# The first stage of an encoder block: x loaded by channels, and the token norm applied after the q, k, v products

## The chip, the cores and the metric

The kernel runs on one core of a Trainium2 chip. The core has TensorE (PE in the profile; its weight loads are listed as PEld), VectorE (DVE), ScalarE (ACT), GpSimd (POOL), a queue engine that issues most transfers (SyncE, SP), and 16 DMA engines. The metric is the device time of one execution in microseconds (us); the median of several runs is compared.

## The reference

One layer of a hybrid encoder block, on 1024 tokens by 1024 channels, in f32. The part that the change touches is its beginning:

```python
h = rms_norm(x, norm_mix[i])                 # y = x * rsqrt(mean(x*x, over channels) + 1e-6); y * gain
proj = h @ w_in[i]                           # 1024 x 4608
q = proj[..., O_Q:O_K].reshape(bsz, s, ATTN_Q_HEADS, HEAD_DIM)      # 512 columns
k = proj[..., O_K:O_V].reshape(bsz, s, ATTN_KV_HEADS, HEAD_DIM)     # 128 columns
v = proj[..., O_V:O_RWKV].reshape(bsz, s, ATTN_KV_HEADS, HEAD_DIM)  # 128 columns
q = rotary_partial(rms_norm(q, q_norm[i]), positions)
k = rotary_partial(rms_norm(k, k_norm[i]), positions)
```

The other columns of `proj` feed an RWKV-7 scan in both directions and two gates per channel. Windowed attention, the scan, the output products, a squared-ReLU MLP and a gated input embedding follow; the change leaves them as they are.

Since the token's factor rsqrt(mean(x*x)+eps) multiplies a whole row of h, it can as well multiply the row of a product: (x * gain) @ w, times the factor, is h @ w.

## The kernel before

Every product of two f32 matrices is taken in three parts: each operand is split into a high part, rounded to the format F32R, and a low part, the difference; then high by high, high by low and low by high are summed in one PSUM bank. `split` (L187) does it for one tile: a copy on ACT makes the high part, a subtraction on DVE or POOL the low one.

The first stage works on 8 token tiles of 128 tokens (t) and 8 channel tiles of 128 channels (k).

- x is loaded by tokens, one 128x1024 tile `xt` for each t (L330). `norm_tile` (L234) takes the sum of squares along the row with one ACT activation (L237), the factor with a small DVE operation (L172) and a power on POOL (L174), and multiplies the tile by factor and gain on DVE (L245).
- TensorE turns the normed tile to channels by tokens: 8 transposes of 128x128, in two groups of four (`tp`, L253). `split` takes each group out of PSUM into `Hh` and `Hl` (L189, L190), which hold the transposed h for two halves of 512 tokens each. All products with w_in read them.
- The weights of q, k and v, 768 columns, come in 8 slices by k (`wqs`, L335) and are split into `wqh` and `wql`, three of the low parts on POOL (`WQP`), five on DVE.
- Token tile t then takes 48 products `psq` (8 k, 2 halves of 384 columns, 3 parts; L439 to L441). Between them stand, at chosen k, the transposes of tile t+1 and those of q and k of tile t-2 (`heads`, L377; `qtp`, L384).
- The result is copied out of PSUM by ACT (`qkv`, L449), v goes to memory (`va_d`, L450), and q and k get a norm by head: squares on ACT (L453), sums on DVE (L455), a power on POOL (`r2`, L458). `rotated` (L395) multiplies, applies the rotation in six small DVE operations, and splits the result; `heads` transposes it, ACT copies it to `qkT` (L386), and POOL issues the transfers to memory (L388, L390).
- After the eighth tile come the first two column blocks of the RWKV part (z12, z13): four sums of 24 products of 128x512 (L218 to L222), with the last two tiles' `heads` between them. Then the preparation of the scan begins with `keys` (first product L230).

The order in which each engine takes its instructions is drawn up ahead of time from the order of the program and from when inputs are planned to be ready; each engine then works through its list in that order and waits at the head of it. `keep_in_program_order` pins an instruction in its place.

## Time and profile before

| what | us |
|---|---|
| median of 3 runs (lowest, highest) | 1730.46 (1728.19, 1732.09) |
| the profiled execution, first to last instruction | 1724.9 |
| PE busy | 1666.1 |
| DVE busy | 1165.3 |
| ACT busy | 879.8 |
| POOL busy | 123.0 |

Busy time of TensorE counts each matmul from its start to its modelled end, though the next one starts before that end; how dense TensorE is, is read from the distance between starts. A start in the timeline is counted from the first instruction of the execution. Of POOL's 123 us the larger part lies in the first 125 us: eight powers of the head norms (15.9 us), eight of the token norms (4.5 us), three low parts of `wql` (6.2 us), four of `wlo` (5.8 us) and 24 transfers to issue (9.4 and 5.8 us).

### The profile page before, as it was taken

To read this page: it belongs to the slowest core of one execution; us is meant where nothing else is said; L and a number is where in the kernel's file an instruction comes from. 1 tells how busy PE (TensorE), PEld (TensorE's weight loads), DVE (VectorE), ACT (ScalarE), POOL (GpSimd) and SP (SyncE) were. 2 spreads that over 40 slices of the span, in tenths; PEclk is the share of its full clock that TensorE was granted. 3 is DMA by queue.
4 is the path that set the end of the run, shared out by engine and by line. 5 is a ranking of instruction groups with operands and counts; after the bars stand their busy time and mean duration, and the time that the engine had idled before them with its cause. 6 is when DMAs were issued, how large, how long until landed. Compare 5 with 4: busy or idle time off the path is not lost.

```text
span 1724.9 us, 29927 instructions
## 1 busy us (share of the span) xinstructions
PE 1666.1 (97%) x11544; PEld 1344.1 (78%) x11544; DVE 1165.3 (68%) x2055; ACT 879.8 (51%) x1620; POOL 123.0 (7%) x148
## 2 busy tenths in 40 slices
PE   7999999899999999998999999999999999999998
PEld 7987777666577878776778878888888888888887
DVE  6658998166948595976763786766667867685342
ACT  5548887277555646464522454444444444554221
POOL 3430000411210000000000100000000000000000
PEclk9999999999999999999999999999999999999999
DMA  6363666846265544456762335444439874574110
GB/s 219 80 151 104 175 184 176 245 130 170 62 183 150 154 138 130 134 168 194 229 223 69 104 119 172 156 140 153 156 132 343 287 218 143 162 222 150 42 40 37
DMA packets 274238, 269.19 MB, mean 156 GB/s; under 512 B 47920, under 2 KB 196272, under 8 KB 274096
## 3 DMA queue, kind: packets, MB, share of 16 engines
q1 hardware_dynamic: 264160, 254.18, 47.6%
q0 software_dynamic: 9792, 12.59, 2.8%
q8 instruction: 91, 1.49, 0.4%
q10 hardware_dynamic: 144, 0.52, 0.1%
q14 instruction: 51, 0.42, 0.1%
HBM read 186.49 MB, written 80.74 MB: 155 GB/s over the span
## 4 chain that ended last, share of the span: by engine, by line
PE 73%; DVE 13%; DMA 6%; ACT 5%; issue 3%; POOL 1%; SPq 0%; DVEq 0%; ACTq 0%; POOLq 0%
PE ff2ps L1793 18%; PE ff1ps L1541 16%; PE gmm L212 3%; DMA wst<-in_w_in_dram 2%; DVE tmp L808 2%; DVE Z L811 2%; PE plps L222 2%; PE plps L218 2%; PE plps L220 2%; PE mm L230 2%; PE mm L232 2%; PE mm L231 2%; PE uaps L212 1%; PE po L943 1%; PE gps L212 1%
## 5 line engine op out<-in xcount | busy, mean ns | idle before, releaser
L1793 PE MATMUL ff2ps<-th,sl 128*128 128x512 f32 x448 | 174.3, 389 | 0.0
L1793 PE MATMUL ff2ps<-tl,sh 128*128 128x512 f32 x448 | 174.3, 389 | 0.0
L1793 PE MATMUL ff2ps<-th,sh 128*128 128x512 f32 x448 | 173.9, 389 | 0.0
L189 ACT CAST sh<-sst 128x512 fp32r<-128x512 f32 x109 | 67.8, 622 | 104.4 <-PE ff2ps L1793 58.7
L190 DVE TENSOR_TENSOR sl<-sst,sh 128x512 fp32r<-128x512 f32 x109 | 75.2, 689 | 47.2 <-ACT sh L189 46.9
L1541 PE MATMUL ff1ps<-mh,w1h 128*128 128x512 f32 x256 | 100.3, 392 | 1.9 <-ACT w1h L189 1.9
L1541 PE MATMUL ff1ps<-ml,w1h 128*128 128x512 f32 x256 | 99.9, 390 | 0.0
L1541 PE MATMUL ff1ps<-mh,w1l 128*128 128x512 f32 x256 | 99.6, 390 | 0.0
L1793 PEld LDWEIGHTS ff2ps<-th,sh 128*128 128x128 f32 x448 | 84.0, 188 | 17.9 <-ACT th L189 0.3
L1793 PEld LDWEIGHTS ff2ps<-tl,sh 128*128 128x128 f32 x448 | 84.1, 188 | 17.5
L1793 PEld LDWEIGHTS ff2ps<-th,sl 128*128 128x128 f32 x448 | 84.1, 188 | 17.4
L189 ACT CAST whi<-wst 128x512 fp32r<-128x512 f32 x100 | 60.4, 617 | 67.7 <-DMA wst<-in_w_in_dram 37.6
L174 POOL TENSOR_TENSOR rstd<-ms,neghalf 128x1 f32<-128x1 f32 x24 | 14.8, 616 | 924.2 <-DVE ms L172 924.2
L189 ACT CAST w1h<-w1st 128x512 fp32r<-128x512 f32 x48 | 28.3, 620 | 98.8 <-DMA w1st<-in_w_ff_dram 58.9
L190 DVE TENSOR_TENSOR w1l<-w1st,w1h 128x512 fp32r<-128x512 f32 x48 | 31.7, 687 | 50.8 <-ACT w1h L189 50.8
L190 DVE TENSOR_TENSOR wlo<-wst,whi 128x512 fp32r<-128x512 f32 x72 | 48.5, 687 | 22.7 <-ACT whi L189 22.4
L1541 PEld LDWEIGHTS ff1ps<-mh,w1h 128*128 128x128 f32 x256 | 48.1, 188 | 12.9 <-ACT w1h L189 2.8
L218 PE MATMUL gmm<-hh,whi 128*128 128x512 f32 x136 | 55.6, 409 | 2.5 <-ACT whi L189 2.5
L1541 PEld LDWEIGHTS ff1ps<-mh,w1l 128*128 128x128 f32 x256 | 48.1, 188 | 10.8 <-DVE w1l L190 0.6
L222 PE MATMUL gmm<-hh,wlo 128*128 128x512 f32 x136 | 55.5, 408 | 0.5 <-POOL wlo L190 0.5
L1541 PEld LDWEIGHTS ff1ps<-ml,w1h 128*128 128x128 f32 x256 | 48.1, 188 | 10.0
L220 PE MATMUL gmm<-hl,whi 128*128 128x512 f32 x136 | 55.5, 408 | 0.0
(406 smaller groups left out, 4720.7 us busy)
## 6 DMA issues: line engine op xcount, KB each, us to landing
wst<-in_w_in_dram SPq DMA_DIRECT2D x92, 256.0 KB, 3.4
tst<-in_w_ff_dram SPq DMA_DIRECT2D x80, 256.0 KB, 4.1
w1st<-in_w_ff_dram SPq DMA_DIRECT2D x32, 512.0 KB, 5.0
hid_S<-h SPq DMA_DIRECT2D x64, 256.0 KB, 2.1
sst<-hid_S SPq DMA_DIRECT2D x64, 256.0 KB, 2.7
hid_A<-h SPq DMA_DIRECT2D x48, 256.0 KB, 2.3
sst<-hid_A SPq DMA_DIRECT2D x45, 256.0 KB, 3.8
ra_d<-ra SPq DMA_DIRECT2D x8, 1024.0 KB, 5.9
```

The costliest lines, as they stand in the source:

```text
L189: a = nc.scalar.copy(hi, src)
L190: b = (lo_eng or nc.vector).tensor_tensor(out=lo, in0=src, in1=hi.bitcast(F32), op=ALU.subtract)
L212: tc.keep_in_program_order(nc.tensor.matmul(*a, **kw))
L218: mm(ps, ah, bh, start=(i == 0), stop=False)
L220: mm(ps, ah, bl, start=False, stop=False)
L222: mm(ps, al, bh, start=False, stop=(i == n - 1))
L230: nc.tensor.matmul(ps, ah, bh, start=(i == 0), stop=False)
L231: nc.tensor.matmul(ps, ah, bl, start=False, stop=False)
L232: nc.tensor.matmul(ps, al, bh, start=False, stop=(i == n - 1))
L808: nc.vector.tensor_tensor(out=tv, in0=Lp[:, t + 1:32, t:t + 1].broadcast_to([P, n, m]), in1=Z[:, t:t + 1, 0:m].broadcast_to([P, n, m]), op ...
L1541: nc.tensor.matmul(ps, x_[:, k, :], y_[:, k, :], start=start and k + i == 0, stop=k == 3 and i == 2, skip_group_check=True)
L1793: nc.tensor.matmul(banks[bs][i], x_[:, isl], y_, start=fresh and p + j == 0, stop=p == NPR - 1 and j == 2, skip_group_check=True)
```

## The change

x is also laid out by channels on the host (`xT`), and loaded in 16 slices of 128 channels by 512 tokens, so that no transpose of x is left. A slice is multiplied by the gain of its channels alone and split at once (`gained`: high part on ACT, low part on DVE); q, k and v are taken from that. For the first three token tiles (`NA`) the products run by k, all three tiles for one k before the next; the other five run tile by tile (`tile_of`).

The sums of squares come from squares on ACT that are added up over k on POOL (`squared`, into `acc`, which has one buffer for both halves), and four small products with a column of ones per half (`stats`), which give the factor of each token. The factor goes onto v (ACT), into the head norm's mean of squares as its square (`rq`), and into the head norm's factor (`qk_norm`).

z12 and z13 and all later products still take the normed h. For them the factors are put on a diagonal (`dg`, DVE), spread to all partitions by a 128x512 product with ones (`spread`, `rB`), multiplied with x and gain (`scaled`, DVE, reading `rB` from PSUM), and split again into `Hh` and `Hl` (`normed`: ACT, and the low part on POOL for the first half, on DVE for the second).

The q and k transposes of tiles 0 to 2 stand in tiles 5 to 7, those of tiles 3 to 6 in the four sums of z12 and z13, and those of tile 7 behind these. Transposes, sums and `psq` share six PSUM banks.

```diff
@@ -125,6 +125,8 @@
     out = {"pc": np.ascontiguousarray(np.concatenate([cols[n] for n in PC], 0).T)}
     out["wa2"] = np.ascontiguousarray(np.concatenate([a["w2"], a["a2"]], 1).transpose(1, 0, 2))
     out["qkn"] = np.ascontiguousarray(np.concatenate([np.tile(a["q_norm"], 8), np.tile(a["k_norm"], 2), a["sink"]])[None])
+    out["xT"] = np.ascontiguousarray(a["x"].T.reshape(KT, P, T).transpose(1, 0, 2))
+    out["gcol"] = np.ascontiguousarray(a["norm_mix"].reshape(KT, P).T)
...
@@ -321,64 +323,153 @@
     QW = pool(sQ, "wqkv")
     PMM = pool(sMM, "psA", space=PSUM, side="right")
     with ExitStack() as s0:
-        A0 = pool(sA, "x0", bufs=2)
+        A0 = pool(sA, "x0")
         PT0 = pool(s0, "ps0", space=PSUM)
-        xts, wq = [], []
...
+        XT = [A0.tile([P, KT, 512], F32, name="xt0"), PY.tile([P, KT, 512], F32, name="xt1", tag="yk")]
+        acc, wq = [], []
+        gcol = QW.tile([P, KT], F32, name="gcol")
+        nc.scalar.dma_start(gcol, I["gcol"])
+        ones = A0.tile([P, P], F32, name="ones")
+        nc.vector.memset(ones, 1.0)
+        def pinned(ins):
+            tc.keep_in_program_order(ins)
+            return ins
+        def load_x(h, k):
+            nc.sync.dma_start(XT[h][:, k], I["xT"][:, k, 512 * h:512 * h + 512])
+        def gained(h, k):
+            pinned(nc.scalar.activation(out=Hh[h][:, k], in_=XT[h][:, k], func=AF.Copy, scale=gcol[:, k:k + 1]))
+            pinned(nc.vector.scalar_tensor_tensor(out=Hl[h][:, k], in0=XT[h][:, k], scalar=gcol[:, k:k + 1], in1=Hh[h][:, k].bitcast(F32),
+                                                  op0=ALU.mult, op1=ALU.subtract))
+        def squared(h, k):
+            if k == 0:
+                acc.append(A0.tile([P, 512], F32, name="acc", bufs=1))
+                pinned(nc.scalar.activation(out=acc[h], in_=XT[h][:, k], func=AF.Square))
+            else:
+                sq = A0.tile([P, 512], F32, name="sq", bufs=2)
+                pinned(nc.scalar.activation(out=sq, in_=XT[h][:, k], func=AF.Square))
+                nc.gpsimd.tensor_tensor(out=acc[h], in0=acc[h], in1=sq, op=ALU.add)
+        def load_wq(k):
+            st = QW.tile([P, 768], F32, name="wqs", bufs=2) if k % 3 == 0 else QW.tile([P, 768], F32, name="wqs", tag="qkv", bufs=4)
             hi = QW.tile([P, 768], F32R, name=f"wqh{k}")
             lo = QW.tile([P, 768], F32R, name=f"wql{k}")
-            split(hi, lo, st, nc.gpsimd if k in WQP else nc.vector, pin=k < WQPIN)
+            for g in range(2) if k == 0 else (slice(None),):
+                gs = slice(384 * g, 384 * g + 384) if k == 0 else g
+                nc.sync.dma_start(st[:, gs], w_in[:, k, 0:768][:, gs])
+                pinned(nc.scalar.copy(hi[:, gs], st[:, gs]))
+                b = (nc.gpsimd if k in WQP else nc.vector).tensor_tensor(out=lo[:, gs], in0=st[:, gs], in1=hi[:, gs].bitcast(F32), op=ALU.subtract)
+                if k not in WQP:
+                    pinned(b)
             wq.append((hi, lo))

-        load_x(0, nc.sync)
-        ident = const("ident", [P, P])
-        gain = A0.tile([P, DM], F32, name="gain", bufs=1)
-        nc.scalar.dma_start(gain, I["gains"][0:1, :].partition_broadcast(P))
-        def normed(t):
-            xs = norm_tile(A0, xts[t], gain, t, 1 if t else 2, pin=t in SQPIN)
+        NA = 3
+        pss = {}
+        def psq_k(t, k):
             h, tq = divmod(t, 4)
             tsl = slice(tq * P, (tq + 1) * P)
...
-        first = normed(0)
+            if k == 0:
+                pss[t] = [PT0.tile([P, 384], F32, name="psq", tag="psq", bufs=6) for _ in range(2)]
+            ah, al = Hh[h][:, k, tsl], Hl[h][:, k, tsl]
+            for g in range(2):
+                gs = slice(384 * g, 384 * g + 384)
+                nc.tensor.matmul(pss[t][g], ah, wq[k][0][:, gs], start=(k == 0), stop=False)
+                nc.tensor.matmul(pss[t][g], al, wq[k][0][:, gs], start=False, stop=False)
+                nc.tensor.matmul(pss[t][g], ah, wq[k][1][:, gs], start=False, stop=(k == KT - 1))
+        rs, rq = [], []
+        def stats(h):
+            st = PMM.tile([P, 4], F32, name="st", tag="mm", bufs=2)
+            for i in range(4):
+                nc.tensor.matmul(st[:, i:i + 1], acc[h][:, i * P:(i + 1) * P], ones[:, 0:1], start=True, stop=True)
+            ms, r, q = (QW.tile([P, 4], F32, name=n, bufs=2) for n in ("ms", "rx", "rq"))
+            nc.vector.tensor_scalar(out=ms, in0=st, scalar1=1.0 / DM, scalar2=EPS, op0=ALU.mult, op1=ALU.add)
+            nc.gpsimd.tensor_tensor(out=r, in0=ms, in1=neghalf.broadcast_to([P, 4]), op=ALU.pow)
+            nc.vector.scalar_tensor_tensor(out=q, in0=r, scalar=1.0 / 64, in1=r, op0=ALU.mult, op1=ALU.mult)
+            rs.append(r)
+            rq.append(q)
+        rB = {}
+        dgs = {}
+        def dg(h):
+            dgs[h] = A0.tile([P, 4, P], F32, name="dg", tag="sq", bufs=2)
+            nc.vector.tensor_tensor(out=dgs[h], in0=ident.unsqueeze(1).broadcast_to([P, 4, P]), in1=rs[h].unsqueeze(2).broadcast_to([P, 4, P]), op=ALU.mult)
+        def spread(h):
+            rB[h] = PMM.tile([P, 512], F32, name="rB", tag="mm", bufs=2)
+            nc.tensor.matmul(rB[h], ones, dgs[h].rearrange("p a t -> p (a t)"), start=True, stop=True)
+        def scaled(h, ks):
+            for k in ks:
+                nc.vector.scalar_tensor_tensor(out=XT[h][:, k], in0=XT[h][:, k], scalar=gcol[:, k:k + 1], in1=rB[h], op0=ALU.mult, op1=ALU.mult)
+        def normed(h, ks, lo_eng):
+            for k in ks:
+                nc.scalar.copy(Hh[h][:, k], XT[h][:, k])
+                a = lo_eng.tensor_tensor(out=Hl[h][:, k], in0=XT[h][:, k], in1=Hh[h][:, k].bitcast(F32), op=ALU.subtract)
+                if lo_eng is nc.gpsimd:
+                    pinned(a)
         for k in range(KT):
...
+            load_x(0, k)
+            if k == 0:
+                gained(0, 0)
+            load_wq(k)
+            if k:
+                gained(0, k)
+            squared(0, k)
+            for t in range(NA):
+                psq_k(t, k)
+        ident = const("ident", [P, P])
...
-        nc.sync.dma_start(qkn, I["qkn"].partition_broadcast(P))
-        for t in range(2, NT):
-            load_x(t, nc.sync)
+        for k in range(KT):
+            load_x(1, k)
+            if k == 3:
+                nc.sync.dma_start(qkn, I["qkn"].partition_broadcast(P))
         gqk = qkn[:, 0:640].rearrange("p (h d) -> p h d", d=64)
         NQK = NH + 2
-        parts = []
+        parts, qkvs, normed_qk = {}, {}, {}
+        def evict(t):
+            qkvs[t] = QW.tile([P, 768], F32, name="qkv", bufs=4)
+            for g in range(2):
+                pinned(nc.scalar.copy(qkvs[t][:, 384 * g:384 * g + 384], pss[t][g]))
+        def qk_norm(t):
+            h, tq = divmod(t, 4)
+            qkv = qkvs[t]
+            r1 = rs[h][:, tq:tq + 1]
+            nc.scalar.activation(out=qkv[:, 640:768], in_=qkv[:, 640:768], func=AF.Copy, scale=r1)
+            nc.sync.dma_start(va_d[t * P:(t + 1) * P, :], qkv[:, 640:768])
+            qk = qkv[:, 0:640].rearrange("p (h d) -> p h d", d=64)
+            qn = QW.tile([P, NQK, 64], F32, name="qsq", tag="wqs", bufs=2)
+            nc.scalar.activation(out=qn, in_=qk, func=AF.Square)
+            ss = QW.tile([P, NQK], F32, name="ss2", bufs=2)
+            nc.vector.tensor_reduce(out=ss, in_=qn, axis=AX.X, op=ALU.add)
+            nc.vector.tensor_scalar(out=ss, in0=ss, scalar1=rq[h][:, tq:tq + 1], scalar2=EPS, op0=ALU.mult, op1=ALU.add)
+            r = QW.tile([P, NQK], F32, name="r2", bufs=2)
+            pinned(nc.gpsimd.tensor_tensor(out=r, in0=ss, in1=neghalf.broadcast_to([P, NQK]), op=ALU.pow))
+            nc.vector.tensor_scalar_mul(r, r, r1)
+            normed_qk[t] = (qk, r)

         def heads(t):

             q2, k4 = parts[t]
             for q in range(3):
-                tp = PT0.tile([P, 4, P], F32, name="qtp", tag="tp0", bufs=2)
+                tp = PT0.tile([P, 4, P], F32, name="qtp", tag="psq", bufs=6)
                 for j in range(4):
                     src = q2[:, 4 * q + j, :, :] if q < 2 else k4[:, j // 2, j % 2, :, :]
                     nc.tensor.transpose(tp[:, j, :], src.bitcast(F32), ident)
@@ -389,8 +480,6 @@
                 else:
                     nc.gpsimd.dma_start(kT_d[:, :, :, t * P:(t + 1) * P], qkT.rearrange("p (a b) t -> p a b t", a=2))
                 yield
-        normed_qk = []

         def rotated(t):

@@ -417,74 +506,77 @@
             for j in range(2):
                 nc.scalar.copy(k4[:, :, 0, j, :], kt)
                 nc.vector.tensor_tensor(out=k4[:, :, 1, j, :], in0=kt, in1=k4[:, :, 0, 0, :].bitcast(F32), op=ALU.subtract)
-            parts.append((q2, k4))
-        for t in range(NT):
-            tps = second if t + 1 < NT else iter(())
-            hps = heads(t - 2) if t > 1 else iter(())
-            order = {**{k: tps for k in TPAT}, **{k: hps for k in HDAT}} if t else {0: tps, 3: tps}
-            if t == NT - 1:
-                sA.close()
-                PW = pool(sW, "wA", side="right")
-                rotated(NT - 2)
-                order = {0: hps, 2: hps, 4: hps}
-            h, tq = divmod(t, 4)
-            tsl = slice(tq * P, (tq + 1) * P)
-            qkv = QW.tile([P, 768], F32, name="qkv", bufs=2)
-            pss = [PT0.tile([P, 384], F32, name="psq", bufs=4) for _ in range(2)]
+            parts[t] = (q2, k4)
+        for t in range(NA):
+            evict(t)
+        for k in range(KT):
+            gained(1, k)
+            squared(1, k)
+        def tile_of(t, hooks):
             for k in range(KT):
...
+                psq_k(t, k)
+                for f in hooks.get(k, ()):
+                    f()
+            evict(t)
+        def head_hooks(t, at, hooks=None):
+            it = heads(t)
+            hooks = dict(hooks or {})
+            for k in at:
+                hooks[k] = [*hooks.get(k, ()), lambda: next(it, None)]
+            return hooks
+        tile_of(3, {2: [lambda: stats(0), lambda: dg(0)], 6: [lambda: spread(0)]})
+        qk_norm(0)
+        scaled(0, range(KT))
+        normed(0, range(2), nc.gpsimd)
+        qk_norm(1)
+        rotated(0)
+        normed(0, range(2, 4), nc.gpsimd)
+        tile_of(4, {7: [lambda: stats(1), lambda: dg(1)]})
+        qk_norm(2)
+        rotated(1)
+        normed(0, range(4, 6), nc.gpsimd)
+        qk_norm(3)
+        tile_of(5, head_hooks(0, (3, 5, 7), {4: [lambda: spread(1)]}))
+        normed(0, range(6, KT), nc.gpsimd)
+        rotated(2)
+        qk_norm(4)
+        scaled(1, range(KT))
+        tile_of(6, head_hooks(1, (1, 4, 6)))
+        rotated(3)
+        qk_norm(5)
+        sA.close()
+        PW = pool(sW, "wA", side="right")
+        tile_of(7, head_hooks(2, (1, 4, 6)))
+        rotated(4)
+        qk_norm(6)
+        normed(1, range(KT), nc.vector)
+        zs = [[], []]
+        wz = [load_w(PW, "w", w_in[:, :, c0:c0 + P], P, parts=2) for c0 in (O_RWKV + 1536, O_RWKV + 1664)]
+        def low_z(h, i, hooks):
+            ps = PT0.tile([P, 512], F32, name="z", tag="psq", bufs=6)
+            zs[i].append(ps)
+            whl = wz[i]
+            for j, _ in enumerate(mm3_steps(ps, [(whl[0][:, k, :], whl[1][:, k, :], Hh[h][:, k, :], Hl[h][:, k, :]) for k in range(KT)])):
+                if j % 6 == 5:
+                    for it in hooks:
+                        next(it, None)
+        low_z(0, 0, [heads(3)])
+        rotated(5)
+        qk_norm(7)
+        low_z(0, 1, [heads(4)])
+        rotated(6)
+        low_z(1, 0, [heads(5)])
+        rotated(7)
+        low_z(1, 1, [heads(6)])
+        for _ in heads(7):
             pass
...
+        z12, z13 = zs
     sQ.close()

     gmask = const("gmask", [P, ND, P])
...
```

74 lines of the change are left out of this document (1 added, 73 removed).

## The prediction

> **What bounds the kernel now.** I read the page first, then the chain of waits in order of time for the first stage, then the timeline of TensorE there.
>
> ```profile
> span 1724.9 us, 29927 instructions
> PE 73%; DVE 13%; DMA 6%; ACT 5%; issue 3%; POOL 1%; SPq 0%; DVEq 0%; ACTq 0%; POOLq 0%
> ```
>
> Nearly three quarters of the chain are TensorE. The stage that changes is the first 122.64 us; in it the chain begins so (start, length):
>
> ```profile
> 0.74 5.33 DMA xt<-in_x_dram
> 6.09 1.16 ACT xs L237 x2
> 7.51 0.57 POOL rstd L174
> 8.10 3.04 DVE xs L245 x2
> 11.19 1.13 PE tp L253 x4
> ...
> 28.55 0.44 PE tp L253 x4
> ...
> 86.04 0.43 PE tp L253 x4
> ```
>
> The norm of the first tile stands ahead of everything: load, squares, power, scaling, transpose. After that the chain is TensorE itself, with the groups of x transposes (28.55 to 86.04, 12 of them) lying on it at 0.44 us each. TensorE's rows for that stage (start, length):
>
> ```profile
> 11.95 0.67 PE L439 MATMUL psq<-wqh,hh 128*128 128x384 f32 x1
> 13.38 0.52 PE L440 MATMUL psq<-wql,hh 128*128 128x384 f32 x1
> 13.70 0.52 PE L441 MATMUL psq<-wqh,hl 128*128 128x384 f32 x1
> 16.90 0.44 PE L439 MATMUL psq<-wqh,hh 128*128 128x384 f32 x1
> 20.33 0.34 PE L440 MATMUL psq<-wql,hh 128*128 128x384 f32 x1
> 21.06 1.07 PE L253 MATMUL tp<-ident,xs 128*128 128x128 f32 x8 [0.40 <-DVE xs L245]
> 21.88 0.42 PE L441 MATMUL psq<-wqh,hl 128*128 128x384 f32 x1
> 48.41 0.33 PE L440 MATMUL psq<-wql,hh 128*128 128x384 f32 x1
> 48.59 0.34 PE L441 MATMUL psq<-wqh,hl 128*128 128x384 f32 x1
> 95.96 0.39 PE L218 MATMUL mm<-hh,whi 128*128 128x512 f32 x1
> 108.14 0.66 PE L384 MATMUL qtp<-ident,k 128*128 128x128 f32 x4 [1.58 <-ACT qkT L386]
> 122.64 0.40 PE L230 MATMUL mm<-hh,whi 128*128 128x512 f32 x1
> ```
>
> The products begin at 11.95, go at half rate until about 16.90 (0.32 us from 13.38 to 13.70) and later at 0.18 (48.41 to 48.59; 0.173 on the average), and except for 21.06 and 108.14 nothing waits. So TensorE bounds the stage, and what leaves its list, or lets it start sooner, shortens the stage. Whether that lasts depends on what comes next (columns of this view: PE, PEld, DVE, ACT, POOL busy):
>
> ```profile
> 160.00:280.00 120.00, 119.95 (x533) 93.70 (x529) 111.22 (x137) 104.01 (x146) 0.00 (x0) 1.00 0.59 169
> ```
>
> Some 533 products, mostly 512 wide at 0.23 us apart, fill 120 us: TensorE is full there too, with DVE at 111 of 120 close behind. A shift at 122.64 is therefore carried to the end, but DVE work left over from the first stage is not absorbed easily.
>
> **The change, part by part.**
>
> *Earlier start.* The bytes moved early on are in the DMA view of 0 to 32 us (40 slices of 0.8 us, GB/s), and the small costs in these rows:
>
> ```profile
> GB/s 0 0 82 200 394 333 327 364 380 415 419 419 388 131 77 227 367 411 215 249 361 304 275 362 335 369 405 410 282 348 195 56 0 26 179 323 190 158 152 333
> L189 ACT CAST whi<-wst 128x512 fp32r<-128x512 f32 x100 | 60.4, 617 | 67.7 <-DMA wst<-in_w_in_dram 37.6
> 10.56 0.84 ACT L189 CAST wqh<-wqs 128x768 fp32r<-128x768 f32 x1
> 8.77 1.81 POOL L190 TENSOR_TENSOR wql<-wqs,wqh 128x768 fp32r<-128x768 f32 x1 [0.70 <-ACT wqh L189]
> ```
>
> The first x slice and half a weight slice are 448 KB; the GB/s row reaches that by about 4.0 us. Then 0.62 for the high part, 0.42 for half of `wqh`, and, ahead of the third product, 0.9 for half of `wql` on POOL and some 0.5 of hand-over: 6.4. Against 11.95 that is **-5.5**. It is -4.0 if the transfers land as late as 5.5, -6.4 if another order hides the low part. The half rate of the first 5 us, some 2.3 us lost (15 products at 0.32 instead of 0.173), is paid in both kernels.
>
> *Can the feed keep up for the first three tiles?* A k takes 18 products at 0.173: 3.1 us (5.8 at half rate). ACT needs 0.62 + 0.62 + 0.84 = 2.1, the transfers 640 KB, about 1.9 us at 330 GB/s. DVE and POOL together: `gained` 0.64 (below), the sum on POOL 1.29, a `wql` on the average 1.25: 3.2 if they exclude each other. Close; the half-rate start gives them 3 us ahead. I put **+0.5**, 0 to 3.
>
> *Transposes of x.* 12 groups at 0.44 are 5.3; the two of tile 1 cost 21.88 - 20.33 less one product's 0.17, 1.4 with their wait. **-6.7**. The two of tile 0 stood before 11.95 and are counted. Their PSUM copies on ACT and DVE go as well, but `gained` has the same sizes.
>
> *The wait at 108.14.* TensorE stood 1.58 us for the last tiles' head chain. With transposes of tiles 3 to 7 spread over four sums it need not: **-1.6**, 0 if it only moves.
>
> *Statistics and spread.* Eight products of 128x128 by one column, two of 512 columns, all plain f32, which this trace doesn't hold. The nearest rows: a transpose, 0.11 each (0.44 for four), and a product of 512, 0.23: 1.4 in all. From below 0.3, from above four times 1.4, 5.6. I take **+2.0**, near the nearest row. (The Trainium skill, "FP8 and Floating Point Precision", section TensorE Precision Notes, says true FP32 takes four passes: by it the two wide ones alone would be an estimated 1.9, the term 1.9 to 2.8 and the sum below -5.6 to -4.7. No run so far shows it.)
>
> These give -11.3: TensorE would reach `keys` at 111.3 if nobody kept it waiting.
>
> *The waits that come in.* That is the real question, because DVE and POOL get more to do, in a shorter time. The rows:
>
> ```profile
> 91.41 3.13 POOL L190 TENSOR_TENSOR wlo<-wst,whi 128x512 fp32r<-128x512 f32 x2
> 91.46 1.92 DVE L399 TENSOR_TENSOR qn<-qkv,r 128x640 f32<-128x640 f32 x1 [2.60 <-POOL r L458]
> 93.42 1.80 DVE L400 TENSOR_TENSOR qn<-qn,qkn 128x640 f32<-128x640 f32 x1
> 103.70 0.83 DVE L399 TENSOR_TENSOR qn<-qkv,r 128x640 f32<-128x640 f32 x1 [2.16 <-POOL r L458]
> 107.84 0.49 DVE L419 TENSOR_TENSOR k<-qn,k 128x128 fp32r<-128x128 f32 x2
> 100.52 0.82 DVE L455 TENSOR_REDUCE ss<-qsq 128x10 f32<-128x640 f32 x1 [2.36 <-ACT qsq L453]
> 19.63 1.28 DVE L245 SCALAR_TENSOR_TENSOR xs<-xt,rstd,gain 128x1024 f32<-128x1024 f32 x1 [0.67 <-POOL rstd L174]
> 316.04 1.29 POOL L190 TENSOR_TENSOR wlo<-wst,whi 128x512 fp32r<-128x512 f32 x1 [0.94 <-ACT whi L189]
> 101.69 1.98 POOL L458 TENSOR_TENSOR r<-ss,neghalf 128x10 f32<-128x10 f32 x1 [0.19 <-DVE ss L456]
> ```
>
> A subtraction on POOL is 1.29 us alone. Beside two of them, DVE's operation of 0.83 takes 1.92 and 1.80: each stood still while POOL worked. So where both have two operands in SBUF, their times add. Now DVE's list from the first `stats` on, at 6.4 + 0.5 + 2.3 (half rate) + 8 x 18 x 0.173 (24.9) + 18 products of tile 3 (3.1) + 0.3 for `stats` itself, 37.5: `rotated` 103.70 to 108.33 less its 0.68 wait, 3.95, eight times, 31.6; head sums 0.82 + 2 x 0.17, eight times, 9.3; `gained` of the second half 8 x 0.64 (half of 1.28), 5.1; `scaled` 16 x 0.64, 10.2; `normed` of the second half 5.1; `dg` and small ones 2.0. Sum 63.3, and 37.5 + 63.3 = 100.8 is below 111.3. But POOL does 7 sums, 8 low parts of `normed` and 4 of `wlo` in that time, 19 x 1.29 = 24.5. Two thirds of DVE's list (`rotated`, `gained`, `normed`) have two SBUF operands, so I let two thirds of it stand in DVE's way: 16.3, end 117.1. TensorE waits **+5.8** instead, at the q and k transposes that `rotated` feeds (first those of tile 0 in tile 5). Bounds: 0, if the DVE work falls between POOL's, and 14.2, if all 24.5 count (125.5).
>
> Queued behind a late POOL sum is more than DVE: `stats` of the second half stands in TensorE's list in tile 4, and `qT_d`, `kT_d` transfers are issued by POOL behind its arithmetic; behind ACT's pinned squares stand its copies of tile 3. SP's transfers come earlier or are no larger than before; `scan` waits for the second x half's buffer, until some 90 us, and is first used past 130, so nothing.
>
> Sum: -5.5 + 0.5 - 6.7 - 1.6 + 2.0 + 5.8 = **-5.5**: a span of 1719.4. The runs' median lies 5.56 above the span; with that unchanged, **1725.0**.
>
> **The rivals.**
>
> *No wait to speak of* (DVE takes its operations between POOL's): -11.3, **1719.2**. For it: in the rows of before DVE has gaps of 2 us behind each power on POOL. Against: 63.3 us of DVE work and 42 of POOL's (24.5, eight powers at 1.98, two small ones) in 74 us.
>
> *The second half's statistics come late.* POOL's list from 37.5 to them: 7 sums 9.0, two head powers 4.0, four low parts 5.2 if they are put between: done near 56, while TensorE asks in the eighth step of tile 4, near 52 (37.5 + 30 products 5.2 + `spread` 0.9 + 48 products 8.3). TensorE then waits some 3.5 more on top of the forecast: -2.0, **1728.5**. For it: the sum can't even begin before `stats` of the first half frees `acc`. Against: TensorE's list can have tile 5 ahead.
>
> *Slower: all of POOL's time stands in DVE's way.* up to `rotated` of tile 0 DVE has 17.5 (`gained` 5.1, `scaled` 5.1, `rotated` 3.95, two head sums 2.3, small ones 1.0), and with eight of POOL's operations in its way (10.3) that is done near 65, while TensorE gets to its transposes near 56, in order; waits of this size recur and DVE ends at 125.5, +2.9 against 122.64. In the one place where TensorE waited 7.3 us at once, its clock fell:
>
> ```profile
> 335.66 7.29 DMA qT<-qT_d
> 340.00:360.00 20.00, 16.64 (x72) 11.95 (x73) 11.28 (x45) 9.86 (x32) 3.32 (x4) 0.79 0.62 191
> ```
>
> 0.79 for 20 us is 4.2 us more. Together +7.1: **1737.6**. It decides from where all waits together exceed 11.3 us. The Trainium skill speaks for this one: "SBUF — State Buffer", section Who interferes with whom, has DVE and GpSimd share a port pair as an exclusive lock, so that the second one stands still until the first is done. By that rule, the trace agrees (1.92 for 0.83); an operation with one operand in PSUM would not be held, which takes `scaled` and the sums out of it.
>
> **How the numbers follow.** Chances: forecast 0.42 (alone 1721.5 to 1728), no waits 0.22, late statistics 0.20, slower 0.16. A measurement of this kernel can tell about 0.2%, 3.5 us, from no change: faster means under 1727.0. Of the forecast 0.36 lies there, of no waits 0.22, of late statistics 0.04: faster 0.62. Slower, over 1733.9, is most of the last case: 0.14. The rest, 0.24, is within. The range takes in the no-wait case and late statistics with their spread and leaves out the far ends: 1718.5 to 1732.5.
>
> **What would show it.** First product at 5.5 to 8 us; no `tp` of x; `keys` at 111 to 122 instead of 122.64; waits of TensorE for `qkT`, DVE or POOL from tile 4 on, at the q and k transposes; DVE operations beside POOL's sums at twice their length; small products well under 3 us in all. Wrong would be: a feed of the first three tiles that starves TensorE for more than 3 us, transposes that wait though DVE is idle, or a shift at `keys` that is gone by 280 because DVE there is late.

## The result, and the profile after

The changed kernel takes 1742.34 us (median of 4 runs, 1740.26 to 1750.65), the kernel before, run beside it, 1731.28: a ratio on record of 1.0091 [1.0072, 1.0111]. The quotient of these two medians is 1.0064; by either the kernel is slower. The forecast was 1725.0, with 1718.5 to 1732.5 as its range; the time lies outside it, on the other side. The profiled execution of the changed kernel took 1744.35 us, 2.0 above its median. From its page:

```profile
span 1742.6 us, 29933 instructions
PE 63%; DVE 14%; DMA 6%; ACT 6%; issue 3%; POOL 1%; SPq 0%; DVEq 0%; ACTq 0%; POOLq 0%
```

TensorE's share of the chain that ended last went from 73% to 63%, but that is no measure of the loss: the shares add up to 93%, since this chain can be followed back only to 126.25 us, past most of the stage that changed. TensorE's timeline for the first stage (start, length, and in brackets what it waited for):

```profile
6.22 0.69 PE L383 MATMUL psq<-wqh,hh 128*128 128x384 f32 x1 [6.22 <-ACT wqh L365]
37.15 0.95 PE L393 MATMUL st<-ones,acc 128*128 128x1 f32 x8
57.48 2.08 PE L411 MATMUL rB<-dg,ones 128*128 128x512 f32 x2 [2.95 <-DVE dg L407]
65.03 0.95 PE L393 MATMUL st<-ones,acc 128*128 128x1 f32 x8
101.53 0.40 PE L220 MATMUL z<-hh,whi 128*128 128x512 f32 x1
134.56 0.48 PE L232 MATMUL mm<-hh,whi 128*128 128x512 f32 x1
151.48 0.91 PE L214 MATMUL px<-lr,wlrh 128*128 128x512 f32 x2
```

The beginning is as hoped: the first product at 6.22 instead of 11.95, and `stats` of the first half at 37.15. From there to `keys` (L232) everything is lost: 134.56 instead of 122.64, +11.9. By the first product of the next stage, `px` (before at 133.72), it is +17.8, and the span ends +17.7. The medians differ by 11.1 only. Each profile is one execution: that of the kernel before has a span 6.4 us under the median of 1731.28, that of the changed kernel one 0.3 above its median, and this makes up the other 6.6. What TensorE waited for up to 160 us:

```profile
PE psq L383 <- ACT wqh L365: 6.2, 1, 6.2
PE psq L384 <- DVE hl L345: 4.1, 4, 2.2
PE qtp L475 <- DVE q L503: 3.8, 1, 3.8
PE rB L411 <- DVE dg L407: 2.9, 1, 2.9
PE qtp L475 <- ACT qkT L477: 2.8, 2, 1.8
PE mm L232 <- ACT z L641: 2.2, 1, 2.2
PE z L220 <- ACT qkT L477: 1.1, 1, 1.1
```

Without the first (the load, there before too) and the sixth (behind `keys`) that is 14.7 us. The waits also cost clock. Windows of before, then of after (columns: PE, PEld, DVE, ACT, POOL busy, granted clock, DMA share, GB/s):

```profile
40.00:70.00 30.00, 30.00 (x194) 29.49 (x193) 20.60 (x51) 17.86 (x38) 12.66 (x15) 1.00 0.35 87
```

```profile
40.00:50.00 10.00, 7.40 (x39) 6.40 (x37) 8.06 (x6) 6.92 (x12) 9.61 (x7) 0.98 0.01 2
50.00:60.00 10.00, 5.57 (x13) 3.56 (x13) 8.43 (x16) 3.98 (x11) 3.16 (x2) 0.50 0.09 27
60.00:70.00 10.00, 10.00 (x53) 10.00 (x53) 8.59 (x13) 6.14 (x11) 8.63 (x6) 0.83 0.00 0
80.00:90.00 10.00, 7.42 (x37) 7.42 (x38) 10.00 (x22) 3.13 (x7) 5.40 (x5) 0.83 0.47 114
```

TensorE was full before; now it stands in three of these stretches, and from 50 to 60 its clock is halved. One less the clock, times 10, summed over the four, is 8.6 us, at most, since some of it falls into waits. What holds it is seen on POOL and DVE, side by side:

```profile
41.88 11.36 POOL L356 TENSOR_TENSOR acc<-acc,sq 128x512 f32<-128x512 f32 x7
```

```profile
41.94 1.25 DVE L465 TENSOR_SCALAR r<-r,rx 128x10 f32<-128x10 f32 x1 [1.94 <-POOL r L464]
43.11 0.81 DVE L461 TENSOR_REDUCE ss<-qsq 128x10 f32<-128x640 f32 x1
43.84 1.25 DVE L345 SCALAR_TENSOR_TENSOR hl<-xt,gcol,hh 128x512 fp32r<-128x512 f32 x1
45.01 1.91 DVE L488 TENSOR_TENSOR qn<-qkv,r 128x640 f32<-128x640 f32 x1
46.84 3.45 DVE L345 SCALAR_TENSOR_TENSOR hl<-xt,gcol,hh 128x512 fp32r<-128x512 f32 x2
53.87 0.74 DVE L345 SCALAR_TENSOR_TENSOR hl<-xt,gcol,hh 128x512 fp32r<-128x512 f32 x1
56.74 0.68 DVE L407 TENSOR_TENSOR dg<-ident,rx 128x512 f32<-128x512 f32 x1
```

While POOL adds the squares of the second half, each low part `hl` on DVE takes 1.25 to 1.75 us, and 0.74 once POOL is done (53.87). Tile 4 on TensorE needs these low parts at that very time, and `dg` for the first `rB` comes only behind the last of them. One more group, of 40 to 125 us:

```profile
L465 DVE TENSOR_SCALAR r<-r,rx 128x10 f32<-128x10 f32 x8 | 5.9, 741 | 9.6 <-POOL r L464 9.6
```

Eight products of 128x10 hold DVE for 15.5 us: 9.6 in which it stands until POOL's root comes, and 0.74 each, where the shortest of them took 0.22.

### The profile page after: what moved, and what is told of

Its sections match the earlier page's. It is cut to its first block, busy times and chain, and to the rows that moved or that the text cites. A ratio compares the mean times of both kernels' runs of the same rounds, so it can differ in the third digit from the quotient of the medians.

```text
span 1742.6 us, 29933 instructions
## 1 busy us (share of the span) xinstructions
PE 1671.5 (96%) x11500; PEld 1344.8 (77%) x11500; DVE 1190.4 (68%) x2077; ACT 890.5 (51%) x1645; POOL 154.7 (9%) x165
## 4 chain that ended last, share of the span: by engine, by line
PE 63%; DVE 14%; DMA 6%; ACT 6%; issue 3%; POOL 1%; SPq 0%; DVEq 0%; ACTq 0%; POOLq 0%
PE ff1ps L1633 17%; PE ff2ps L1885 15%; PE gmm L214 3%; DMA wst<-in_w_in_dram 2%; DVE tmp L900 2%; DVE Z L903 2%; PE plps L224 2%; PE plps L220 2%; PE plps L222 2%; PE po L1035 1%; PE gps L214 1%; PE uaps L214 1%; DMA g1t<-g_d 1%; PE mmo L234 1%; PE mmo L232 1%
## 5 line engine op out<-in xcount | busy, mean ns | idle before, releaser
L176 POOL TENSOR_TENSOR rstd<-ms,neghalf 128x1 f32<-128x1 f32 x16 | 10.1, 633 | 895.9 <-DVE ms L174 895.9
L1633 PEld LDWEIGHTS ff1ps<-mh,w1h 128*128 128x128 f32 x256 | 48.1, 188 | 12.3 <-ACT w1h L191 2.2
```

What stands on the lines that cost most here:

```text
L1633: nc.tensor.matmul(ps, x_[:, k, :], y_[:, k, :], start=start and k + i == 0, stop=k == 3 and i == 2, skip_group_check=True)
```

## The experiments

Keys and px are the starts of those first products in the profiled run; the time is a median; the ratio is to the kernel before, run on the same chip. The runs were taken on several chips, the changed kernel's time is the median of four executions that spread over 10 us, and the gains at `px` told below are 1 to 4 us larger than those of the medians (e1 7.4, e2 9.1, e8 11.2, e14 9.4 against the changed kernel). So the size of a step is known to some 3 us, not to a tenth. The time of e11 counts one execution of 8442 us, which its ratio leaves out; without it the median is 1728.61.

| run | keys | px | time (before) | ratio, 95% |
|---|---|---|---|---|
| before | 122.64 | 133.72 | | |
| changed kernel | 134.56 | 151.48 | 1742.34 (1731.28) | 1.0091 [1.0072, 1.0111] |
| e1 second half first | 128.56 | 144.08 | 1738.87 (1730.82) | 1.0046 [1.0027, 1.0066] |
| e2 without second sums | 126.76 | 142.36 | 1737.01 (1730.82) | 1.0038 [1.0024, 1.0051] |
| e3 ones by memset | 134.77 | 150.23 | 1741.76 (1730.82) | 1.0061 [1.0038, 1.0084] |
| e4 low parts on DVE | 134.46 | 153.29 | 1745.88 (1730.82) | 1.0085 [1.0059, 1.0110] |
| e7 other sequence | 131.52 | 146.81 | 1739.86 (1729.75) | 1.0062 [1.0038, 1.0086] |
| e8 without second norming | 123.49 | 140.28 | 1734.91 (1729.75) | 1.0030 [1.0015, 1.0045] |
| e9 second half dealt out | 126.90 | 142.47 | 1735.51 (1729.75) | 1.0035 [1.0022, 1.0048] |
| e10 = e8, order of z | 123.49 | 140.83 | 1734.37 (1729.75) | 1.0034 [1.0013, 1.0054] |
| e11 = e9 and fold | 118.85 | 135.00 | 1729.37 (1729.51) | 0.9998 [0.9985, 1.0011] |
| e12 = e9 without second norming | 117.66 | 132.96 | 1728.55 (1729.51) | 0.9999 [0.9987, 1.0011] |
| e13 = e11, roots first | 121.07 | 136.37 | 1728.95 (1729.51) | 0.9992 [0.9980, 1.0004] |
| e14 fold alone | 126.29 | 142.06 | 1735.69 (1729.27) | 1.0043 [1.0023, 1.0064] |
| e15 = e11, low-rank loads early | 119.77 | 136.39 | 1729.72 (1729.27) | 1.0005 [0.9992, 1.0017] |
| e16 = e11, last heads early | 119.45 | 132.49 | 1725.34 (1728.61) | 0.9978 [0.9963, 0.9994] |
| e17 = e16, order of z | 120.59 | 132.87 | 1726.62 (1728.61) | 0.9992 [0.9979, 1.0004] |

**e1: the second half prepared ahead of the evicts, with two sum tiles.**

```diff
-acc.append(A0.tile([P, 512], F32, name="acc", bufs=1))
+acc.append(A0.tile([P, 512], F32, name="acc", bufs=2))
-        for t in range(NA):
-            evict(t)
         for k in range(KT):
             gained(1, k)
             squared(1, k)
+        for t in range(NA):
+            evict(t)
```

> Two buffers for acc, and gain, split and squares of the second half of x placed ahead of the copies of the first three tiles, so that they run from about 25 us on, while TensorE still works on tiles 0 to 2. Theory A (the second half is prepared too late, at 38 to 57 us, because its squares wait for the one acc buffer; TensorE then starves in tile 4 and its clock halves): tile 4's waits for hl (4.1 us) and for dg (2.9 us) go, the clock stays at 1.00 from 40 to 70 us, some 10 to 14 us faster than the changed kernel, about 1729 to 1733. Theory B (DVE has too much work in all, whenever it comes): the waits move to the q and k transposes, at most 4 us faster, about 1738.

3.5 us less than the changed kernel. Its longest waits of TensorE between the load and `keys`:

```profile
PE qtp L475 <- ACT qkT L477: 4.7, 5, 2.2
PE rB L411 <- DVE dg L407: 2.7, 1, 2.7
PE psq L383 <- ACT qkv L449: 2.6, 1, 2.6
PE psq L383 <- ACT qkT L477: 2.0, 1, 2.0
```

No wait for `hl` is left, but tile 3 now waits for the evict of an earlier tile and the transposes for `qkT`. The late preparation is a cause, and only a part of the loss: the time is what theory B said, `px` lies between the two.

**e2: without POOL's seven sums of the second half.**

```diff
-nc.gpsimd.tensor_tensor(out=acc[h], in0=acc[h], in1=sq, op=ALU.add)
+if h == 0:
+    nc.gpsimd.tensor_tensor(out=acc[h], in0=acc[h], in1=sq, op=ALU.add)
```

> Leaves out the seven additions on POOL for the second half's sums of squares (its token factors are then wrong); squares on ACT, order and buffers as in the changed kernel. Theory P (POOL's additions hold DVE's operations with two SBUF operands): the eight hl of the second half take 0.74 us each instead of up to 1.9, tile 4 waits less than 2 us in all instead of 7, and the time falls by 8 us or more, to about 1734. Rival (ACT's pinned chain sets the pace, gain and square in turn, whatever POOL does): hl still comes every 1.3 us, about 3 us faster, about 1739.

5.3 us less, and the waits for `hl` are gone: each low part takes 0.74 or 0.75 us on DVE again, so they were late because of POOL's sums. The waits for `q` (4.1) and `dg` (2.6) stay, and the gain is less than the 8 us of theory P.

**e3: the constant of ones by memsets.** Around `keys` the changed kernel's queue and DVE show this:

```profile
129.18 6.94 SPq L208 DMA_DIRECT2D wst<-in_w_in_dram  x4
136.17 0.49 SPq L598 DMA_DIRECT2D one<-in_one_dram  x1
```

```profile
142.61 0.23 DVE L599 CAST one_r<-one 128x128 fp32r<-128x128 f32 x1 [6.30 <-DMA one<-in_one_dram]
```

and the kernel before this, 9.6 us ahead of its `keys`:

```profile
113.07 0.59 SPq L506 DMA_DIRECT2D one<-in_one_dram  x1
```

```diff
-nc.sync.dma_start(one, I["one"])
+nc.vector.memset(one, 0.0)
+for b in range(2):
+    nc.vector.memset(one[64 * b:64 * b + 64, 64 * b:64 * b + 64], 1.0)
```

> The block of ones for the scan's preparation is made by three memsets on DVE instead of a transfer that stands in SP's queue behind weights. Theory S (DVE's queue stands 6.3 us at 136 to 142.6 for this transfer, and the first px product with it): px comes at about 145 to 147 instead of 151.5, 4 to 6 us faster, about 1737. Rival (the two lr weights, which are loaded behind it, take its place): less than 2 us, about 1741.

`px` gains 1.3 us, the time 0.6, less than a measurement tells: the loads of the low-rank weights stand behind the same four on SP's queue, and DVE waits 2.7 us for those.

**e4: the first half's low parts of `normed` on DVE in place of POOL.**

```diff
-normed(0, range(2), nc.gpsimd)
+normed(0, range(2), nc.vector)
...
```

> The eight low parts of the normed first half go to DVE instead of POOL. Theory P (POOL's subtractions hold DVE at 61 to 82 us; one q of rotated took 3.52 us instead of 0.68): the 3.8 us wait at 82.6 and the half clock from 80 to 90 us go, 4 to 8 us faster, about 1735 to 1738. Rival B (DVE has too much to do): 8 x 0.68 = 5.4 us more on DVE delay the q and k transposes, slower by up to 4 us, about 1746.

3.5 us more, near the rival's number: waits for `q` of 5.7 us and for `dg` of 5.6. Taking POOL out of DVE's way by giving DVE its work doesn't pay.

**e7 and e9: sequences.** e9 has two sum tiles, memsets for the ones, and deals the preparation out; e7 in addition moves the second half's statistics and `spread` into tile 3 beside those of the first, `rotated` of tiles 0 and 1 ahead of `scaled(0)`, the low parts of `normed(0)` into two groups of four, and the head transposes in tile 5 one or two steps forward.

```diff
         for k in range(KT):
             gained(1, k)
             squared(1, k)
+            if k in (3, 5, 7):
+                evict((3, 5, 7).index(k))
```

> What is tried: the sequence of the changed kernel, with two sum tiles, the second half's gained and squared dealt out between the three evicts (after k = 3, 5 and 7), and the constant of ones by two memsets. Where the early half alone gave 1738.9 and its new wait was tile 3's wait for the evict of tile 0 (2.6 us), this takes that wait away. Theory O: waits for hl and for that evict go, rB's wait for dg stays at some 2.7 us, and the time is 1734 to 1737. Theory W: the waits move on to tiles 4 and 5, and the time is 1738 to 1742.

> What is tried: two sum tiles (acc), the second half's gained and squared placed between the evicts of tiles 0 to 2, its statistics already in tile 3, both spreads at the end of tile 3, rotated(0) ahead of scaled(0), the constant of ones written by two memsets in place of its load. Theory O (the sequence makes the loss: the second half's statistics come too late, and dg, spread and the rotated heads stand behind them in VectorE's list): the waits for hl, dg and q go from 10.8 us to under 3 us, the clock stays above 0.95 from 40 to 90 us, keys starts at 117 to 122, and the time is 1726 to 1732. Theory W (VectorE and GpSimd have too much work in all between 40 and 115 us, in any order): the waits move to other tiles, keys stays at 127 or later, and the time is 1736 to 1741.

e9 has no wait for `hl` or the evict any more and takes 6.3 us less than e3, in the middle of what the theory of the sequence said. e7, from which that theory expected more, is worse: waits for `qkT` of 12.3 us. ACT, which copies `qkT`, stands 4.2, 5.1 and 3.1 us in front of `q` until DVE's rotation is done (at 73.47, 89.65 and 97.98), and DVE's 128x10 product of the head norm takes 4.93 us at 78.03, beside four of POOL's low parts in a row (77.89 to 82.92). An order on paper isn't enough; something in the heads' chain is slow.

**e8 and e12: without the second norming**, alone and with e9's order.

```diff
-tile_of(3, {2: [lambda: stats(0), lambda: dg(0)], 6: [lambda: spread(0)]})
+tile_of(3, {2: [lambda: stats(0)]})
-scaled(0, range(KT))
-normed(0, range(2), nc.gpsimd)
...
```

> What is left out: the second norming of x (dg, spread, scaled, normed for both halves), so that z and all later products take x times the gain without the token norm; q, k and v are as before. Theory W (the second norming is the work that is too much): the waits for dg (2.9 us) and for q (3.8 us) go, keys starts at 118 to 122 against 134.6, and the time is 1726 to 1731, at the kernel before or under it. Theory O: the waits for hl (4.1 us, at 45 to 54 us) stay as they are, since POOL's sums and VectorE's low parts of the second half stay; the clock falls there all the same, keys starts at 124 to 128, and the time is 1733 to 1737. Both say that the waits for hl stay; they differ in what follows behind 56 us.

> What is left out: the second norming (dg, spread, scaled, normed), and with it the waits for the second half's low parts, by two sum tiles and by dealing the second half's preparation between the evicts of tiles 0 to 2; the constant of ones comes from memsets. Dealing it out alone brought keys from 134.6 to 126.9, leaving the norming out alone brought it to 123.5. Theory S (the two causes add up: the unprepared second half, and the second norming): keys at 115 to 118, the clock at 1.00 from 40 to 90 us, and the time 1725 to 1730, under the kernel before. Rival (one pool of lateness: with either gone VectorE's chain of the heads is what is left): keys at 121 to 124, waits of qtp for qkT or q of 6 us or more, and the time 1732 to 1735.

7.4 us less alone, 7.0 on top of e9: within the error told above the two add up. What the norming costs in work is seen up to `keys`, in the windows of before, of the changed kernel and of e8:

```profile
0.00:122.64 122.64, 110.56 (x640) 104.03 (x641) 73.55 (x162) 65.51 (x125) 47.19 (x51) 1.00 0.55 156
```

```profile
0.00:134.56 134.56, 113.60 (x593) 103.49 (x593) 95.92 (x168) 72.31 (x143) 77.71 (x65) 0.94 0.41 122
```

```profile
0.00:123.49 123.49, 109.04 (x588) 102.43 (x589) 76.48 (x142) 63.85 (x127) 66.86 (x57) 0.96 0.44 133
```

DVE is busy 22.4 us longer than before, the time that POOL holds it included, and POOL 30.5; without the norming DVE is busy 2.9 longer. And yet e12, which leaves that work out, is no faster than the kernel before, though its `keys` starts 5.0 us earlier; its `px` is 0.8 ahead.

**e14, e11, e13: the token's factor folded into the head norm.** With s the head's mean square, m the token's and f = m^(-1/2), the change takes (s f^2 + EPS)^(-1/2) and then times f on DVE, which is (s + EPS m)^(-1/2), in one step.

```diff
-nc.vector.scalar_tensor_tensor(out=q, in0=r, scalar=1.0 / 64, in1=r, op0=ALU.mult, op1=ALU.mult)
+nc.vector.tensor_scalar_mul(q, ms, EPS)
-... in0=ss, scalar1=rq[h][:, tq:tq + 1], scalar2=EPS, ...
+... in0=ss, scalar1=1.0 / 64, scalar2=rq[h][:, tq:tq + 1], ...
-nc.vector.tensor_scalar_mul(r, r, r1)
```

> What is tried: the changed kernel with the token's factor folded into the heads' norm and nothing else. With the second half dealt out the fold brought 6 us (1735.5 to 1729.4). Theory C (the chain of each tile's heads costs by itself): the wait of qtp for q (3.8 us) and those for qkT (2.8 us) shrink by half or more, the time is 1735 to 1738. Rival (the waits for hl and dg at 45 to 57 us set the rest of the stage back whatever the heads' chain does): the wait for q stays over 2 us, the waits for hl and dg stay as they are (7 us), and the time is 1739 to 1742.

> What is tried: the kernel with the second half dealt out, and the token's factor folded into the heads' norm: each head's square mean is not scaled by rq and its root then multiplied by rx, but EPS times the mean square is added instead of EPS, so that the root is at once the whole factor; eight small VectorE products and one step of each tile's chain fall away. In the run with the second half dealt out VectorE stood 9.8 us before these eight products, until POOL's root came. Theory C (the chain of each tile, with POOL's root behind POOL's low parts, sets when the heads are there): waits of qtp for qkT and q fall from 8.9 us to some 5 us and the time is 1731 to 1734. Rival (the root itself comes late whatever follows it): the wait goes over to qn's first product, and the time is 1734 to 1737.

6.6 us less alone, as theory C had it, and 6.1 on top of e9, more than it had there. The wait didn't go over to the next product; DVE's first use of the root, in e14:

```profile
L487 DVE TENSOR_TENSOR qn<-qkv,r 128x640 f32<-128x640 f32 x8 | 8.7, 1084 | 2.9 <-POOL r L464 2.5
```

2.5 us of standing in place of 9.6. The small product had its place in DVE's list right behind POOL's root, and DVE stood in front of it with `hl`, `scaled` and `rotated` of other tiles behind; without it, seven of the eight first uses of the root come late enough in the list to find it ready. Part of the gain may be the 5.9 us of the products themselves. In e14 the waits for `q` are gone and those of the transposes for `qkT` down to 1.4, while those for `dg` (5.3, from 2.9) and `hl` (2.6, from 4.1) together stay near their 7 us, as the rival had it.

> What is tried: as the run with the token's factor folded in, and beside it another sequence: each tile's norm chain with POOL's root comes ahead of POOL's low parts of the second norming, which go two by two behind tiles 4, 5, 6 and into the gap before tile 7, and VectorE's scaled is cut into halves behind the rotations. Theory C: the roots no longer stand behind 2.5 to 3.2 us of POOL's low parts, waits of qtp fall under 3 us, keys starts at 117 to 121, and the time is 1726 to 1731. Rival (VectorE's amount of work decides, 22 us more than before ahead of keys): the waits move to scaled and to z's operands, keys stays at 124 or later, and the time is 1733 to 1737.

e13, with another sequence, is not told apart from e11.

**e10, e15, e16, e17: the handover to the next stage.** In e11 `keys` starts 3.8 us ahead of the kernel before, and `px` 1.3 us behind it.

> What is left out: the second norming, as in the run without it; beside it the four low-rank sums run in the order of the kernel before (first weight pair for both halves, then the second pair). From keys to the first product of px the kernel before takes 11.1 us and the changed kernel 16.9. Theory Z (the changed order of the sums frees the weight buffers one sum later, so that the loads of ones and of the low-rank weights stand behind on SP's queue): this stretch comes back to 11 to 12 us, and the time is 3 to 5 us under the run without the second norming alone. Rival (what follows is saturated, and only the place of the wait moves, as when the load of ones was removed): the stretch shortens, but the time is within 1.5 us of that run.

The order of the four sums has no part (e10 against e8). e15 loads the low-rank weights into a tile that is free early:

```diff
-st = A1.tile([P, ND, 512], F32, name="wlrst", tag="th", bufs=3)
+st = nrm[:, i].rearrange("p (d n) -> p d n", d=ND)
```

> What is tried: the kernel with the second half dealt out, the constant of ones by memsets and the token's factor folded in, and beside it the two loads of the low-rank weights land in a buffer that is free early (nrm) in place of one that comes free only with the last heads. In the run without this VectorE stood 3.9 us at 125.9 for that load, and the first product of px came 16.2 us behind keys. Theory H (the handover to the next stage gives back what keys gains): VectorE's wait goes, px comes 11 to 13 us behind keys, at 130 to 132, and the time is 1725 to 1727.5, under the kernel before by 0.1 to 0.3 per cent. Rival (px's lateness is taken up by keys' products, and what follows is bound elsewhere): px comes earlier, the time stays at 1728.5 to 1730.

DVE's wait for the load is gone, but ACT now stands at 131.54 for a weight cast that needs `keys`' sums done, ahead of the activation that the chain to `px` needs:

```profile
131.54 0.62 ACT L191 CAST whi<-wst 128x512 fp32r<-128x512 f32 x1 [4.90 <-PE mm L233]
132.06 1.05 ACT L651 ACTIVATE z<-z 64x1024 f32<-64x1024 f32 x1
```

So `px` came no earlier, and the run says nothing of what an earlier `px` is worth. e16 puts the last tile's head transposes into the fourth sum in place of behind it:

```diff
-if j % 6 == 5:
+if j % every == every - 1:
...
-low_z(1, 1, [heads(6)])
-for _ in heads(7):
+low_z(1, 1, [heads(6), h7], 3)
+for _ in h7:
```

> What is tried: the kernel with the second half dealt out, ones by memsets and the factor folded in, and beside it the last tile's heads are transposed inside the fourth low-rank sum (a step behind every third product) in place of behind it. Theory G (the next stage begins when the last heads are evicted, which before was 6.6 us ahead of keys and in that run 2.1 us behind it): ScalarE's first zr comes at keys or up to 2 us ahead of it, px comes 13 to 14.5 us behind keys, and the time is 1726 to 1728.5. Rival (the heads are not ready earlier, TensorE waits for q or qkT inside the sum): keys moves back by what px would win, and the time is 1729 to 1732.

```profile
119.45 0.40 PE L232 MATMUL mm<-hh,whi 128*128 128x512 f32 x1
```

```profile
132.49 0.73 PE L214 MATMUL px<-lr,wlrh 128*128 128x512 f32 x2 [0.65 <-DVE lr L656]
```

`px` comes 13.0 us behind `keys`, and the kernel takes 1725.34, 0.9978 [0.9963, 0.9994] of the kernel before: the one version of sixteen whose interval lies below 1, and barely, so that its gain is not secured. The theory's detail did not hold: ACT's first `zr` comes at 122.05, 2.6 us behind `keys`, as in e11 (2.1). `px` waits for the last `lr`, and its 2.5 us are seen on DVE, in e11 and then in e16:

```profile
129.82 0.69 DVE L628 CAST wlrh<-wlrst 128x1024 fp32r<-128x1024 f32 x1 [3.90 <-DMA wlrst<-in_wa_dram]
133.73 1.22 DVE L654 TENSOR_TENSOR lr<-z,lr 64x1024 fp32r<-64x1024 f32 x1
```

```profile
128.76 0.69 DVE L630 CAST wlrh<-wlrst 128x1024 fp32r<-128x1024 f32 x1 [0.64 <-DMA wlrst<-in_wa_dram]
131.22 1.22 DVE L656 TENSOR_TENSOR lr<-z,lr 64x1024 fp32r<-64x1024 f32 x1
```

The low-rank weights are there 1.1 us earlier, and from them to that `lr` it is 2.5 us instead of 3.9, since in e11 two casts for the second half (at 132.41 and 133.01) stand ahead of it and in e16 behind.

> What is tried: as the run with the last heads inside the fourth sum, and beside it the four low-rank sums in the order of the kernel before (the first weights for both halves, then the second). Theory Z (the first weights' buffer comes free one sum earlier, so the loads behind it on SP's queue go earlier): px comes 11 to 13 us behind keys and the time is 1725 to 1727. Rival (the first sum of the second half now needs its normed x 5.6 us earlier, or the order has no part, as without the second norming): the time is within 1.5 us of the run without this order, or above it.

Again within 1.5 us of the run without that order, and no longer told apart from the kernel before, though the last heads stand early here too.

## Why the prediction was wrong

*Earlier start*, -5.5: measured 6.22 - 11.95 = -5.7. *The feed*, +0.5: `stats` was put to end at 37.5; it began at 37.15 and ended by 37.96, with TensorE waiting for nothing from 6.22 on. *Transposes of x* are gone, as counted. These three held.

*Statistics and spread*, +2.0: `stats` is eight instructions for four products and takes 0.81 (37.15 to 37.96) per half. `rB` is two; at full clock, in e9, it starts at 43.18 and the second product behind it at 44.31, so less the 0.17 of the one between it cost 0.96. Together 3.5, inside the bounds. The Trainium skill ("FP8 and Floating Point Precision", section TensorE Precision Notes) has four passes for true FP32, by which an estimated 4 x 0.23 = 0.92 for each wide product: e9 agrees, the nearest row (0.23) did not.

*The wait at 108.14*, -1.6: it did not go. There are waits for `qkT` of 2.8 us, in the same place (107.88) and later.

*The waits that come in*, +5.8 with bounds 0 and 14.2: this is the step that failed. It summed DVE's work, added two thirds of POOL's, and let TensorE wait only at the end, as if an engine always had something to do. Measured were 14.7, just past the upper bound (which by its own terms, 37.5 + 63.3 + 24.5 = 125.3, should read 14.0), and they begin at 45 us. Of these, 6.6 are at the q and k transposes, where the sum had put its 5.8; 7.0 are waits of tile 4 for `hl` and of the spread for `dg`, for which it had no term. The lock between DVE and POOL was as assumed for operations with two operands in SBUF (0.74 alone, up to 1.75 beside POOL); a reduction beside POOL was not held, as assumed, while the small products with 128x10 were (1.25), which was not. The runs took the loss apart into three pieces, of about the same worth within their error: the second half's preparation falls on POOL's sums just when tile 4 needs it (e9 against e3, 6.3 us), the second norming's work (e8, 7.4), and DVE standing idle in its own list behind POOL's root, with the small products that stand there (e14, 6.6; 9.6 us of standing). The sum had the second one in its total; it had no term for the first and the third. The last was in plain sight, since the kernel before shows waits of 2 us and more for that root too; there TensorE did not wait for DVE meanwhile (1.6 us in all from 22 us on, and that for ACT). The prediction read these gaps as slack that speaks for no waits, when they were DVE's time lost.

*The clock* was left out of the forecast, at nothing. With the measured terms, -5.7 - 6.7 + 0.6 (stage to `stats`, 30.9 against 30.3) + 3.5 + 14.7 less the 1.6 that the wait at 108.14 was before: +4.8; measured is +11.9, so some 7 us are left for the lower clock, of the 8.6 that the windows allow. That is a remainder and no measurement of its own, but the same sum with the waits and the clock of other runs comes out near as well: 127.5 for `keys` in e9 (11.4 of waits and 3.4 of clock; measured 126.90) and 118.2 in e16 (3.8 and 1.7; 119.45).

*What comes next.* "SP's transfers come earlier or are no larger than before", so nothing: wrong. `keys` to `px` takes 16.9 us against 11.1, with the ones and the low-rank weights issued 23 us later than before, 1.6 us behind `keys` in place of 9.6 ahead. Moving one load away only moved the wait (e3); e16 shows that some 3 us of this can be had (13.0 from `keys` to `px`, against 16.2 in e11). That a shift is carried to the end held in the profiles: +17.8 at `px`, +17.7 at the end, and over all 17 profiles the stretch from `px` to the end is 1588.9 to 1596.5 us (1591.2 before). The 5.56 us between span and median, taken over unchanged, belong to the one profiled execution of the kernel before; in the changed kernel the span lies 0.3 above the median.

*The rival.* "Slower: all of POOL's time stands in DVE's way" gave 1737.6 (1737.4 with the sum above) and a chance of 0.16; its turning point, waits of over 11.3 us, was passed and it came out 4.7 below the measured time. Its mechanism was a part: e2 shows the lock at work, but the loss is as much one of order. "The second half's statistics come late" did not happen: POOL's sums were done at 53.24, near the 56 put down for them, but TensorE, held up by `hl` and `dg`, came to these `stats` only at 65.03 and did not wait. "No wait to speak of" was reached by no run: e16 has the fewest waits, 3.8 us, and `keys` at 119.45 where this rival has 111.3; e12, which leaves the norming out, comes to 117.66, and there the handover took the gain.

## What to carry to other kernels

An engine that works through a list in order does not fill its gaps: sum up what it waits for at the head of its list as well as what it has to do, and look for small operations that follow another engine's result. A tiny instruction there can cost more than a large one elsewhere; here eight of 128x10 cost some 6 us of the kernel. When work leaves a full engine and goes to the others, price the waits that come back to it, and a lower clock on top as a range: on 14.7 us of waits some 7 here, on 11.4 us 3.4 in e9, on 3.8 us 1.7 in e16, on 7.0 us nothing in e17. Then follow the gain through the handover to the next stage before it is counted.

## What was not expected of the hardware

- **The clock can fall after short waits, and their length alone does not decide.** In e9 a wait of 2.80 us brought the 10 us around it to 0.83, one of 2.69 brought two such stretches to 0.95 and 0.88, and one of 2.75 left 1.00. In e11 one of 2.19 brought 0.83; in e17 one of 2.32 and in e1 one of 2.64 left 1.00. In e2 waits of 2.62 and 4.14 gave 0.83. Each of those that told cost 1.7 us; in e12 one of 5.87 gave 0.79 and 0.87, 3.4 us lost. What decides between them is open. The Trainium skill ("TensorE: Matmul & The Clock Gate", Part 1) lets the clock fall to half after at least one idle window of about 3.4 us; half of such a window is an estimated 1.7, the loss measured, but here waits shorter than a window were enough, and not always.
- **The lock also holds tiny operations.** The 128x10 product with one column as its factor took 1.25 us beside POOL's sums (0.22 at the shortest), while a reduction of 128x640 at the same time took its usual 0.81. In e7 it took 4.93 beside four operations of POOL in a row.
